# A decoder trunk on one core: the query norm carried into the exponential's scale, and an output projection of 512 columns

## The chip, the cores and the metric

The kernel runs as one program on one core of one Trainium2 chip. The metric is the time of one execution on the device in microseconds (us); the time before is the median of three runs. The profile is one execution of the same program taken by the hardware profiler. Engines are named as in the profile: PE is the matrix engine, PEld its loading of weights, DVE the vector engine, ACT the scalar engine, POOL the third elementwise engine, SP the queue that issues nearly all transfers.

## The reference

512 prompt rows and 32 sample rows (8 sequences of 4 new tokens) go through a trunk of two layers, D = 1024, 8 heads of 128, FFN width 2816. Layer 0 is FFN, gated token mixer, FFN, gated embedding; after it a shared K/V and a log-forget value for each head and row are made. Layer 1 has attention in the mixer's place. The change lies in layer 1's attention:

```python
q = rmsnorm((xn @ att_w_q[j]).reshape(bsz, L, N_HEADS, HEAD_DIM), q_norm[j])   # norm over each head's 128
...
s = jnp.einsum('bqhd,bkhd->bhqk', qb, k).astype(jnp.float32) * scale           # scale = 128 ** -0.5
s = s + cq[..., :, None] - csum[..., None, :]                                  # summed log-forget
s = jnp.where(causal[None, None], s, -jnp.inf)
p = jax.nn.softmax(s, axis=-1).astype(v.dtype)
o = jnp.einsum('bhqk,bkhd->bqhd', p, v)
mix = o.reshape(bsz, L, D_ATT) @ att_w_o[j]
h = h + mix                                                                    # then FFN on rmsnorm(h)
```

The sample rows attend to 256 cached rows each, in pages, and to their own 4. All of it is float32 at the accuracy of float32.

## The kernel before

Activations stand transposed: `h[c]` holds 128 features (chunk c of 8) by 544 columns, 512 of the prompt and 32 of the sample. Two chunks share one tile (`hp`). A weight matrix comes in units of 128 x 1024, each with a load on SP and a split into two reduced-precision halves, `hi` by an ACT cast (L242) and `lo` by a DVE subtraction (L243). A product is then three matmuls, hi·hi, hi·lo and lo·hi (L286, L290, L292 in `mm`), and these run on two column halves of 272 (`HT`). A product of the sample with raw float32 operands, 32 weight columns wide, stands four abreast in the array (for example L904 in the K/V stage). `prepare` splits a weight unit two or three units ahead of its use.

Layer 1's attention (`attention`) is a list of steps, the string `ORDER`, executed in that order in the source; each step is a letter and a number. A scheduler of the language then places each instruction on its engine by a timeline of its own, so that the order on an engine is not that of the source where dependencies leave room; an engine runs its list strictly in order. The steps:

- `q` head h's query tile (48 matmuls over 8 chunks), evicted by DVE (L1112) with the row norm of the stream, then squared on ACT (L788). `s` adds up the squares of four heads (L796), takes the root, and sends the rows to DRAM and back as a tile over all partitions; `n` multiplies q by it on DVE (L1122); `p` splits q into two halves.
- `f` fetches K and V of a head; `a` (`qk`) is its scores in four blocks of 128 queries, the log-forget terms entering as one more matmul (L1173) of two operands `L` and `R`; behind it stand the maximum (L1188, DVE), the exponential (L1189, ACT), the reciprocal (L1190) and the scaling of the rows (L1192, L1194). `t` transposes the weights (L1204), `v` is the product with V (L1223 to L1225).
- `K`, `V` load cache pages; `z`, `S`, `T`, `P`, `U`, `O` are the sample's attention: `S` scores (L1250), `T` transposes, `P` the product with the cached V (L1289, L1296), picked out by heads on DVE (L1303, L1305), `U` a transpose back (L1309, copied at L1312), `O` the split into the columns of the sample in `o` (L1320, L1321).
- `h` (`project_half`) is the output projection of the first 272 columns for two chunks and four heads at a time, `o` (`project`) that of the other 272 columns for one chunk and all heads. Both read `att_w_o`, in two layouts (`woh`, `wo`), so that its 4 MB are loaded and split twice.

When a chunk of `h` is done, `on_chunk` prepares it for the next FFN: `prep` (L342 on ACT, L343 on DVE), the square for the norm (L369 on ACT, added up on POOL at L371). The next FFN begins with four plain query-like tiles (L286 to L292) and goes on with products of combined blocks (L540) that need `forms`, sums of a pair of chunks (L352, L330 on ACT; L356, L358, L359, L331 on DVE). `early={5: 0, 6: 1}` makes two of the four forms when chunks 5 and 6 are done. PSUM is held in three double tiles (`ps`) and two single ones (`pb`).

## Time and profile before

| what | value |
|---|---|
| runs | 1926.22 us median (1925.88, 1926.22, 1927.91) |
| the profiled execution | 1926.16 us, span 1924.4 us, TensorE clock granted 1.0 |
| PE matmul | 1903.1 us busy (99%), 16508 instructions |
| DVE / ACT / POOL | 1457.2 (76%) / 949.1 (49%) / 142.2 us (7%) |
| chain that ended last | PE 89%, DVE 6%, ACT 3% |
| layer 1's attention | the norm sums of its first query tile (L408) at 1355.2 us, the next FFN's first matmul at 1518.3 us |

The chain of work follows PE from one end to the other. Matmuls overlap: a matmul's record lasts longer than the distance to the next one's start, so what a matmul costs is read from two starts, not from one record's length. Where a stage keeps PE busy without a gap, its time is the number of its matmuls by that distance; where PE waits, the view of waits names for what.

### The profile page before, as it was taken

The numbers are of one execution on the slowest core, as the hardware profiler recorded it, in microseconds if no ns is written. First come the engines' busy times: TensorE is split into PE (matmuls) and PEld (weight loads), VectorE is DVE, ScalarE is ACT, GpSimd is POOL, SyncE is SP. The second block draws the span as 40 slices with busy tenths as digits, with TensorE's granted clock in tenths as the row PEclk, the third lists the DMA queues.
The fourth block names the chain that finished last, engine by engine and source line by source line (L and its number), as shares of the span: only waits on it lengthen the run. The fifth ranks groups of instructions, "written<-read, shape, count | busy, mean of one in ns | idle before, by whom it ended". The sixth has DMA issues, their size and how long they took to land.

```text
span 1924.4 us, 39011 instructions
## 1 busy us (share of the span) xinstructions
PE 1903.1 (99%) x16508; PEld 1869.2 (97%) x16508; DVE 1457.2 (76%) x1801; ACT 949.1 (49%) x1398; POOL 142.2 (7%) x190
## 2 busy tenths in 40 slices
PE   9999999999999999999999999999999999999999
PEld 8999999999999999999999999999977899999999
DVE  7987877556788887767578887876476888878774
ACT  7544434424554544454466444444374754444461
POOL 0000000400100000023000000002131300000020
PEclk9999999999999999999999999999999999999999
DMA  5323235203223233431484232324769332332431
GB/s 197 92 98 125 88 115 165 90 26 110 89 88 116 94 113 121 130 112 50 150 304 148 97 129 71 128 96 128 227 212 333 101 109 86 107 113 86 143 106 47
DMA packets 98048, 237.62 MB, mean 123 GB/s; under 512 B 12130, under 2 KB 29826, under 8 KB 97874
## 3 DMA queue, kind: packets, MB, share of 16 engines
q1 hardware_dynamic: 97730, 235.09, 36.9%
q8 instruction: 130, 2.13, 0.5%
q14 instruction: 44, 0.36, 0.1%
q10 hardware_dynamic: 144, 0.04, 0.0%
HBM read 218.65 MB, written 16.44 MB: 122 GB/s over the span
## 4 chain that ended last, share of the span: by engine, by line
PE 89%; DVE 6%; ACT 3%; issue 1%; DMA 1%; POOL 0%; SPq 0%; ACTq 0%; DVEq 0%; POOLq 0%
PE ps L540 31%; PE ps L286 15%; PE ps L292 15%; PE ps L290 15%; PE pb L540 5%; DVE big L243 1%; ACT big L242 1%; DVE big L227 1%; PE ps L893 1%; PE ps L894 1%; PE ps L895 1%; DMA big<-in_w13p 1%; DVE big L331 0%; DVE big L498 0%; PE ps L1289 0%
## 5 line engine op out<-in xcount | busy, mean ns | idle before, releaser
L540 PE MATMUL ps<-big,big 128*128 128x272 f32 x5616 | 668.7, 279 | 4.0 <-ACT tmp L548 2.6
L540 PEld LDWEIGHTS ps<-big,big 128*128 128x128 f32 x5616 | 658.5, 189 | 5.0 <-ACT tmp L548 3.2
L243 DVE TENSOR_TENSOR big<-big,big 128x1024 fp32r<-128x1024 f32 (+2 forms) x507 | 582.3, 1152 | 87.1 <-ACT big L242 86.4
L242 ACT CAST big<-big 128x1024 fp32r<-128x1024 f32 (+2 forms) x507 | 482.5, 972 | 326.1 <-DVE big L227 253.2
L286 PE MATMUL ps<-big,big 128*128 128x272 f32 x2668 | 530.3, 280 | 3.6 <-ACT big L242 2.3
L292 PE MATMUL ps<-big,big 128*128 128x272 f32 x2668 | 527.6, 279 | 1.4 <-DVE big L243 1.3
L290 PE MATMUL ps<-big,big 128*128 128x272 f32 x2668 | 527.5, 279 | 0.5 <-DVE big L343 0.5
L286 PEld LDWEIGHTS ps<-big,big 128*128 128x128 f32 x2668 | 407.3, 189 | 8.2 <-ACT big L242 5.2
L292 PEld LDWEIGHTS ps<-big,big 128*128 128x128 f32 x2668 | 406.8, 189 | 2.8 <-DVE big L243 2.4
L290 PEld LDWEIGHTS ps<-big,big 128*128 128x128 f32 x2668 | 406.8, 189 | 0.9 <-DVE big L343 0.9
L371 POOL TENSOR_TENSOR st<-st,tmp 128x544 f32<-128x544 f32 (+1 forms) x63 | 87.6, 1391 | 1485.0 <-ACT tmp L369 1484.8
L227 DVE TENSOR_TENSOR big<-big,big 128x1024 f32<-128x1024 f32 x156 | 190.1, 1218 | 0.0
L579 DVE SCALAR_TENSOR_TENSOR big<-ps,big 128x544 f32<-128x544 f32 x128 | 92.4, 722 | 104.1 <-PE ps L292 103.2
L548 ACT COPY tmp<-ps 128x544 f32<-128x544 f32 x117 | 71.5, 611 | 111.3 <-PE ps L540 111.2
L498 DVE TENSOR_TENSOR big<-big,st 128x1088 f32<-128x1088 f32 x88 | 113.2, 1288 | 3.4 <-ACT big L562 2.0
L540 PE MATMUL pb<-big,big 128*128 128x272 f32 x936 | 114.8, 279 | 0.0
L540 PEld LDWEIGHTS pb<-big,big 128*128 128x128 f32 x936 | 111.3, 189 | 0.0
L501 ACT ACTIVATE big<-big 128x544 f32<-128x544 f32 x88 | 57.8, 659 | 87.7 <-DVE big L498 87.6
L342 ACT ACTIVATE big<-big,gains 128x544 fp32r<-128x544 f32 (+1 forms) x80 | 55.5, 702 | 90.0 <-DVE big L579 55.1
L331 DVE TENSOR_TENSOR big<-big,big 128x544 fp32r<-128x544 f32 (+1 forms) x112 | 79.3, 714 | 22.8 <-ACT big L330 22.6
L343 DVE SCALAR_TENSOR_TENSOR big<-big,gains,big 128x544 fp32r<-128x544 f32 (+1 forms) x80 | 64.7, 816 | 23.6 <-ACT big L342 23.4
L330 ACT CAST big<-big 128x544 fp32r<-128x544 f32 (+1 forms) x112 | 71.2, 644 | 12.0 <-DVE big L504 7.4
(218 smaller groups left out, 1385.8 us busy)
## 6 DMA issues: line engine op xcount, KB each, us to landing
big<-in_w SPq DMA_DIRECT2D x156, 512.0 KB
big<-in_w2b SPq DMA_DIRECT2D x96, 384.0 KB
big<-in_w13p SPq DMA_DIRECT2D x16, 512.0 KB
big<-in_w2a SPq DMA_DIRECT2D x16, 512.0 KB
big<-in_win SPq DMA_DIRECT2D x16, 512.0 KB
big<-in_wg SPq DMA_DIRECT2D x16, 512.0 KB
big<-in_ck SPq DMA_DIRECT2D x16, 512.0 KB
big<-in_cv SPq DMA_DIRECT2D x16, 512.0 KB
```

The costliest lines, as they stand in the source:

```text
L227: self.nc.vector.tensor_tensor(t, a, b, ALU.add if op == "+" else ALU.subtract)
L242: self.nc.scalar.copy(hi[:, c], src[:, c])
L243: self.nc.vector.tensor_tensor(lo[:, c], src[:, c], hi[:, c].bitcast(F32), ALU.subtract)
L286: i = nc.tensor.matmul(o, wh, xh[:, b], start=s, stop=False)
L290: nc.tensor.matmul(o, wh, xl[:, b], start=False, stop=False)
L292: nc.tensor.matmul(o, wl, xh[:, b], start=False, stop=e)
L331: self.nc.vector.tensor_tensor(pair[:, 1, cols], src, pair[:, 0, cols].bitcast(F32), ALU.subtract)
L371: nc.gpsimd.tensor_tensor(acc[:, cols], acc[:, cols], sq, ALU.add)
L498: tt(g, g, rstd.unsqueeze(1).broadcast_to([P, 2, T]), ALU.mult)
L540: nc.tensor.matmul(turns(dst[w]), a[:, c], woven(b), start=k in "152" and kp == 0 and n == 0, stop=kp == NKP - 1 and n == 2, skip_group_ch ...
L548: nc.scalar.copy(t["r" + k], t["C" if k == "5" else "A"])
L579: nc.vector.scalar_tensor_tensor(halves(h[c]), whole(out), 0.5, halves(h[c]), ALU.mult, ALU.add)
```

## The change

- The query norm is not applied to q. q goes unnormed, with the gain of the norm alone, into the scores (`prep` in place of `split_pair`). Each query row's factor enters at the exponential as a scale, and the maximum is multiplied by it before. The log-forget terms, which must not be scaled, are divided by it: operand `L` now carries the root of the row and `R` the terms (their parts are exchanged).
- The factor is made in columns: the sums of squares (`s`) are copied to a tile, turned by four transposes (`root`, L1131), and a root is computed on 16 columns by an integer estimate and three rounds of Newton on DVE (L1136 to L1150). `rows` spreads it, transposes it back (L1159) and copies it (L1160) to `L`. For heads 0 to 3, `root` and `rows` are called from within the query tiles 4 and 5, ahead of the last chunk; for heads 4 to 7 they are steps `c1` and `r1`. The trip through DRAM and steps `n`, `z` and `O` are gone; the sample's queries are copied and squared on POOL as each head's tile is evicted.
- Maxima, reciprocals and scalings come for two query blocks at once.
- The projection of the prompt runs on 512 columns, two chunks and four heads at a time (`project`, L1364 to L1368), with one layout of `att_w_o`, loaded and split once. The sample's 32 rows are projected with the raw weights in float32, four abreast (`sample_project`, steps `g`, L1405), copied by ACT (L1409), summed over the four groups by two small matmuls (`sample_add`, steps `e`, L1415) and added by DVE (L1418).
- A chunk counts as done when both parts are in; `on_chunk` then prepares all 544 columns at once. `early={1: 0, 3: 1, 5: 2}`: three forms.
- `ORDER` is written anew: head 0's scores come after query tile 5, and query tiles 6 and 7 stand between the first heads' scores.

```diff
-q0 K3 K2 K0 q1 q2 q3 K1 s0123 n2 n3 n1 q4 f1 p1 q5 q6 f0 n0 q7 p2 p0 f3 f2 a0 s4567 p3 t0 a1 v0 a2
...
-V3 v5 a6 x V2 h10 t6 a7 V4 S1 t7 T0 v6 V0 V1 v7 h20 V6 h30 T1 P0 h01 U0 P1 O0 h11 h21 U1 O1 h31 o0 o1 o2
-o3 o4 o5 o6 o7
+q0 K3 K2 K0 q1 q2 q3 s0 f0 q4 p0 f1 q5 a0 p1 K1 q6 t0 f2 a1 p2 q7 s1 v0 t1 c1 f3 a2 p3 v1 S0 t2 r1 a3
...
+t7 T0 V0 V1 v7 h20 V6 T1
+P0 h30 U0 P1 h01 U1 h110 g0 g1 h111 e0 e1 g2 g3 h210 e2 e3 h211 h31
```

```diff
+                p = self.tile_mm(xs, mid={4: lambda: root(0), 5: lambda: rows(0)}.get(h))
...
+        def stat(g):
+            box["row", g] = row = self.tmp()
+            for a, t in enumerate(self.head_stat([sqs.pop(4 * g + j) for j in range(4)])):
+                nc.scalar.copy(row[:, a * HT:(a + 1) * HT], t[:, :HT])
+        def root(g):
+            dve, n, t, row = nc.vector, 18 if g else 16, self.pb(), box.pop(("row", g))
+            for i in range(4):
+                nc.tensor.transpose(t[:, i * P:i * P + P], row[:, i * P:i * P + P], self.ident)
+            for k in range(2 * g):
+                nc.tensor.matmul(t[:, 1 + k:2 + k], ss[k], self.ones[:, 0:1], start=True, stop=True, skip_group_check=True)
...
+            for _ in range(3):
+                dve.tensor_tensor(u, y, y, ALU.mult)
+                dve.scalar_tensor_tensor(u, u, -0.5, x, ALU.mult, ALU.mult)
+                dve.scalar_tensor_tensor(y, u, 1.5, y, ALU.add, ALU.mult)
...
+            for k, part in enumerate((hi.bitcast(F32), u)):
+                dve.tensor_copy(v[:, :, :, 2 * k:2 * k + 2], part.unsqueeze(2).unsqueeze(3).broadcast_to([P, 16, NH, 2]))
+        def rows(g):
+            w, t = box.pop(("w", g)), self.pb()
+            for i in range(4):
+                nc.tensor.transpose(t[:, i * P:i * P + P], w[:, i * P:i * P + P], self.ident)
+            nc.scalar.copy(self.L[:, g, :SEQ], t)
...
-                nc.tensor.matmul(into, self.L[h % 4][:, qs], blocks_woven(self.R[:, 0, :w]), start=True, stop=False)
+                nc.tensor.matmul(into, self.L[:, h // 4, qs], blocks_woven(self.R[h % 4][:, :w]), start=True, stop=False)
...
-                nc.scalar.activation(blocks_halves(p[:, :w]), blocks_unwoven(sc), AF.Exp, bias=m, accum_out=l)
+                nc.scalar.activation(blocks_halves(p[:, :w]), blocks_unwoven(sc), AF.Exp, bias=m2[:, k], scale=r2[:, k],
+                                     accum_out=l2[:, k])
...
+        def project(c, part, only=None):
+            if only != 1:
+                st["sum", c, part] = self.ps()
+            p = st["sum", c, part]
+            hi, lo, _ = weights(c, part)
+            for a in range(2) if only is None else (only,):
+                w = slice(4 * P * a, 4 * P * a + 4 * P)
+                product(p[:, a, :], (hi[:, w], lo[:, w]), range(4 * part, 4 * part + 4))
+                if part == 1:
+                    out = halves(h_out[2 * c + a][:, :SEQ])
+                    nc.vector.tensor_tensor(out, unwoven(p[:, a, :]), out, ALU.add)
+                    done(c, a)
...
+        def sample_project(c):
+            st["part", c] = t = self.pb()
+            for part in range(2):
+                w = weights(c, part)[2].rearrange("p (a n m) -> p n a m", a=2, n=4)
+                for n in range(4):
+                    nc.tensor.matmul(t[32 * n:32 * n + 32, :2 * P].rearrange("p (a m) -> p a m", a=2),
+                                     st["os"][:, 4 * part + n, :], w[:, n], start=part == 0, stop=part == 1,
+                                     skip_group_check=True)
+            st["own", c] = s = self.tmp()[:, :2 * P]
+            nc.scalar.copy(s, t[:, :2 * P])
+        def sample_add(c):
+            s, t = st.pop(("own", c)), st.pop(("part", c))
+            for a in range(2):
+                nc.tensor.matmul(t[:, 2 * P + NS * a:2 * P + NS * a + NS], s[:, P * a:P * a + P],
+                                 self.c[:, C_SUM:C_SUM + NS], start=True, stop=True, skip_group_check=True)
+            out = self.hp[c][:, :, SEQ:]
+            nc.vector.tensor_tensor(out, t[:, 2 * P:2 * P + 2 * NS].rearrange("p (a t) -> p a t", a=2), out, ALU.add)
+            done(c, 0, 1)
...
-        on, nxt = self.next_norm(h, G_FFN2 + 8, early={5: 0, 6: 1})
+        on, nxt = self.next_norm(h, G_FFN2 + 8, early={1: 0, 3: 1, 5: 2})
```

Ahead of the attention, the two sides issue the same matmuls in the same order.

Three places of the new order matter below. In the rows that follow, a name's number is the buffer.

The first place is on PE where head 0's scores begin. Before, the first matmul of the scores of head 0 (L1173, the log-forget term) stands among the matmuls of a query tile:

```order
L286 MATMUL ps_16809<-big_15947,big_16679 128x272 x2
L290 MATMUL ps_16809<-big_15947,big_16679 128x272 x2
L1173 MATMUL ps_16875<-big_16229,big_16232 128x256
L292 MATMUL ps_16809<-big_15947,big_16680 128x272 x2
L286 MATMUL ps_16809<-big_15965,big_16679 128x272 x2
```

Now the transposes of `rows` (L1159, which read `tmp_16654`) stand behind the last matmul of query tile 5 (`ps_16684`), and the scores (L1210 is the log-forget term, whose weights are `L`, `big_16223`) directly behind them:

```order
L286 MATMUL ps_16684<-big_16216,big_16506 128x272 x2
L290 MATMUL ps_16684<-big_16216,big_16506 128x272 x2
L292 MATMUL ps_16684<-big_16216,big_16507 128x272 x2
L1159 MATMUL pb_16727<-consts,tmp_16654 128x128 x4
L1210 MATMUL ps_16746<-big_16225,big_16223 128x256
```

On DVE the last rows that make `tmp_16654` (L1154) have the eviction of query tile 5 (L1107, from `ps_16684`) between them:

```order
L1148 TENSOR_TENSOR cols<-cols 128x16
L1149 CAST cols<-cols 128x16
L1150 TENSOR_TENSOR cols<-cols 128x16
L1154 COPY tmp_16654<-cols 128x128x2
L1107 TENSOR_TENSOR big_16663<-ps_16684,st_16294 128x544
L1154 COPY tmp_16654<-cols 128x128x2
L343 SCALAR_TENSOR_TENSOR big_16793<-big_16304,gains,big_16793 128x512
```

So four transposes and the copy to `L` now stand between the query tile and the scores, and one of their operands is complete only after the eviction of that same tile.

The second place is on DVE behind the sample's product with V. Before, the picking of the second group (L1303, L1305) follows the copy of the first transpose back (L1312) directly:

```order
L1312 COPY tmp_18336<-pb_18334 128x128
L1303 TENSOR_SCALAR tmp_18363<-ps_18338,consts 128x128
L1305 SCALAR_TENSOR_TENSOR tmp_18363<-ps_18338,consts,tmp_18363 128x128 x7
L1355 TENSOR_TENSOR big_93<-ps_18388,big_93 128x2x272
L1355 TENSOR_TENSOR big_94<-ps_18432,big_94 128x2x272
```

Now an addition of the projection (L1393) stands between its parts, and on PE 13 matmuls of 512 columns stand between the two transposes back (L1346), where 36 of 272 stood before:

```order
L1350 COPY tmp_18288<-pb_18286 128x4x8x4
L1340 TENSOR_SCALAR tmp_18315<-ps_18290,consts 128x128
L1393 TENSOR_TENSOR big_92<-ps_18324,big_92 128x512
L1342 SCALAR_TENSOR_TENSOR tmp_18315<-ps_18290,consts,tmp_18315 128x128 x7
L1393 TENSOR_TENSOR big_92<-ps_18324,big_92 128x512
```

So the second transpose back has less time on PE and one DVE instruction more ahead of it.

The third place is on ACT where the next FFN's first weight unit is cast (L242). Before, that cast stands among the work of the last chunks' second halves (`big_94` is chunks 4 and 5, `big_95` chunks 6 and 7):

```order
L342 ACTIVATE big_18470<-big_94,gains 128x272
L369 ACTIVATE tmp_18757<-big_94 128x272
L330 CAST big_18765<-tmp_18763 128x544
L330 CAST big_18766<-tmp_18764 128x544
L242 CAST big_18775<-big_18691 128x1024
L342 ACTIVATE big_18528<-big_95,gains 128x272
```

Now it comes behind two chunks' preparation, a form, and the copies for the last two sums of the sample (L1409), with chunks 4 to 7 still to be prepared:

```order
L342 ACTIVATE big_18446<-big_93,gains 128x544
L342 ACTIVATE big_18452<-big_93,gains 128x544
L352 ACTIVATE big_18458<-big_93,gains 128x544 x2
L330 CAST big_18463<-tmp_18461 128x544
L1409 COPY tmp_18487<-pb_18472 128x256
L1409 COPY tmp_18504<-pb_18489 128x256
L330 CAST big_18464<-tmp_18462 128x544
L242 CAST big_18477<-big_18329 128x1024
L369 ACTIVATE tmp_18526<-big_94 128x544
```

On PE the last matmuls of the projection, the two pairs L1415 that read `tmp_18487` and `tmp_18504`, and the first matmul of the FFN, which reads `big_18477`, follow one another directly.

More of the change, by code (lines that the diff above doesn't have):

```diff
@@ L1332, in product @@
                 c = slice(P * n, P * n + P)
-                s, e = n == 0, n == len(ks) - 1
-                i = nc.tensor.matmul(turns(out), hi[:, c], woven(o[k][:, 0, hs]), start=s, stop=False)
-                if pin and s:
+                xh, xl = (woven(o[k][:, x, :SEQ]) for x in range(2))
+                i = nc.tensor.matmul(turns(out), hi[:, c], xh, start=n == 0, stop=False)
+                if pin and n == 0:
                     self.tc.keep_in_program_order(i)
-                if not late:
-                    nc.tensor.matmul(turns(out), hi[:, c], woven(o[k][:, 1, hs]), start=False, stop=False)
@@ new lines, in product, with weights, done @@
+                nc.tensor.matmul(turns(out), lo[:, c], xh, start=False, stop=n == len(ks) - 1)
+        def weights(c, part):
+            if ("w", c, part) not in st:
+                hi, lo = self.unit()
+                st["w", c, part] = hi, lo, self.raws[self.pieces[self.p_next - 1]["src"][0]]
+            return st["w", c, part]
+        def done(c, *chunks):
+            for a in chunks:
+                st["done", c, a] = st.get(("done", c, a), 0) + 1
+                if st["done", c, a] == 2:
+                    on_chunk(2 * c + a)
@@ L1371, in attention @@
+        do = dict(q=tile, s=stat, c=root, r=rows, f=fetch, p=prep_q, a=qk, t=turn, v=pv, K=self.load_k, V=self.load_v,
+                  S=sample_qk, T=sample_turn, P=sample_pv, U=sample_back, x=load_vs, h=project,
+                  g=sample_project, e=sample_add)
         for step in ORDER.split():
```

163 lines of the change are left out of this document (73 added, 90 removed).

## The prediction

> **What bounds the kernel now.** The page first: how busy PE is, and whether any other engine comes near it.
>
> ```profile
> span 1924.4 us, 39011 instructions
> PE 1903.1 (99%) x16508; PEld 1869.2 (97%) x16508; DVE 1457.2 (76%) x1801; ACT 949.1 (49%) x1398; POOL 142.2 (7%) x190
> ```
>
> PE is without work for about 21 us of 1924.4. A change can win what of that idleness lies in its own stage, and what it takes off PE itself; anything else is hidden. So the second view is busy time by stretches (core time, then busy us of PE, PEld, DVE, ACT, POOL). The first row is another FFN's beginning, in layer 0; the others run through layer 1's attention and the start of its second FFN.
>
> ```profile
> 540.00:564.00 24.00, 23.27 (x201) 23.04 (x200) 23.49 (x30) 14.84 (x21) 0.00 (x0) 1.00 0.41 132
> 1344.00:1392.00 48.00, 47.71 (x404) 45.13 (x403) 22.39 (x30) 16.68 (x23) 8.39 (x18) 1.00 0.70 210
> 1392.00:1416.00 24.00, 20.58 (x138) 17.17 (x138) 15.73 (x41) 16.81 (x45) 7.56 (x11) 1.00 0.37 127
> 1416.00:1484.00 68.00, 67.15 (x711) 54.99 (x710) 47.92 (x111) 41.63 (x106) 18.75 (x40) 1.00 0.99 327
> 1484.00:1518.00 34.00, 32.20 (x279) 30.99 (x265) 28.71 (x46) 22.12 (x53) 14.22 (x27) 1.00 0.40 135
> 1518.00:1544.00 26.00, 24.29 (x201) 23.37 (x200) 21.77 (x31) 19.33 (x30) 1.90 (x2) 1.00 0.29 101
> 1544.00:1572.00 28.00, 25.34 (x214) 24.77 (x213) 24.91 (x26) 15.95 (x22) 0.00 (x0) 1.00 0.24 76
> ```
>
> Clock column: 1.00 throughout. PE's idleness (first two numbers subtracted) is 0.29 + 3.42 + 0.85 = 4.56 up to 1484, 1.80 to 1518, 1.71 to 1544 and 2.66 to 1572: 10.73 us. That is all that better order can give back. The waits of PE in 1380 to 1572 (us in total, times, longest) say what ended it:
>
> ```profile
> PE ps L1173 <- ACT tmp L1189: 2.6, 4, 1.3
> PE ps L540 <- ACT tmp L548: 1.7, 2, 1.3
> PE ps L292 <- DVE big L243: 1.3, 3, 0.5
> PE ps L1341 <- POOL big L1321: 1.2, 1, 1.2
> ```
>
> The first heads' scores wait for PSUM that exponentials still hold; the FFN's start waits for weight splits and evictions; the last projection waits for POOL's split of the sample's `o`, which the change drops.
>
> **PE's own work.** Prices are distances between starts:
>
> ```profile
> 1369.80 0.40 PE L290 MATMUL ps<-big,big 128*128 128x272 f32 x2
> 1370.03 0.40 PE L292 MATMUL ps<-big,big 128*128 128x272 f32 x2
> ...
> 1399.56 0.38 PE L1174 MATMUL ps<-big,big 128*128 128x512 f32 x1
> 1399.78 0.38 PE L1175 MATMUL ps<-big,big 128*128 128x512 f32 x1
> 1400.00 0.38 PE L1176 MATMUL ps<-big,big 128*128 128x512 f32 x1
> ...
> 978.66 0.28 PE L895 MATMUL ps<-big,big 128*128 128x256 f32 x1
> 978.86 1.07 PE L904 MATMUL pb<-big,xraw 128*32 128x256 f32 x16
> 979.86 0.38 PE L893 MATMUL ps<-big,big 128*128 128x256 f32 x1
> ...
> 927.88 1.18 PE L977 MATMUL pb<-big,tmp 128*128 128x8 f32 x10
> 928.91 0.36 PE L894 MATMUL ps<-big,big 128*128 128x256 f32 x1
> ...
> 1417.83 0.93 PE L1204 MATMUL ps<-consts,tmp 128*128 128x128 f32 x7
> 1418.51 0.46 PE L1223 MATMUL pb<-big,big 128*128 128x512 f32 x1
> ```
>
> - Projection: 384 matmuls of 272 at 0.23 / 2 = 0.116 give 44.5 us; 192 of 512 at 0.22 (0.2165 over the run of them) give 41.6. **-2.9**. The columns fall from 384 x 272 to 192 x 512, by 6%, because the sample's leave.
> - `sample_project`: the sample's columns come back as 32 raw float32 products of 256 columns, four abreast. L904 is the same shape: 16 records are 8 products and take 1.00 us, with about 0.2 around them for coming and going. They stand in two blocks of 16: 2 x (2.0 + 0.2) = **+4.4**.
> - `sample_add`: 8 float32 products with 128 weight columns and 32 moving ones. Nearest is L977, 5 products in 1.03: 0.2 each, 1.6, and 0.2 for changes: **+1.8**. `root`'s two products of one column, the same price: **+0.4**.
> - 16 transposes in four blocks: 7 in 0.68, so 0.1 each, and 0.1 a block for changing: **+2.0**.
>
> PE gets 5.7 us more to do. Bounds: 4.5 if block changes cost nothing, 7 if each small float32 product costs 0.3.
>
> The Trainium skill would price the first item otherwise. Its page "TensorE: Matmul & The Clock Gate", section "Back-to-back issue gap", gives 131 ns for each 512-column matmul in a sustained stream of weight loads and matmuls; by it the projection would be 25.1 us, and the sum 16.4 lower. The trace disagrees: the three L1174 to L1176 rows, each with its own weights, stand 0.22 apart; the measurement decides.
>
> **Waits.** Prices from rows of the stage 1344 to 1572 (mean ns before the last bar), and the rows around the transpose back of the sample:
>
> ```profile
> L1112 DVE TENSOR_TENSOR big<-ps,st 128x544 f32<-128x544 f32 x8 | 5.7, 722 | 10.3 <-PE ps L292 10.3
> L331 DVE TENSOR_TENSOR big<-pb,big 128x256 fp32r<-128x256 f32 x8 | 3.3, 414 | 0.0
> L1228 ACT CAST big<-pb 128x512 fp32r<-128x512 f32 x8 | 4.6, 582 | 5.7 <-PE pb L1225 5.7
> L243 DVE TENSOR_TENSOR big<-big,big 128x1024 fp32r<-128x1024 f32 x36 | 44.5, 1240 | 6.9 <-ACT big L242 6.5 <-DMA big<-in_cv 0.3
> L242 ACT CAST big<-big 128x1024 fp32r<-128x1024 f32 x36 | 37.0, 1040 | 9.5 <-DVE big L227 7.9 <-PE ps L540 1.6
> L352 ACT ACTIVATE big<-big,gains 128x544 f32<-128x544 f32 x8 | 5.5, 739 | 0.0
> L330 ACT CAST big<-tmp 128x544 fp32r<-128x544 f32 x8 | 5.1, 646 | 4.3 <-DVE tmp L359 3.1 <-DVE tmp L356 1.0
> ...
> 1485.90 0.27 PE L1309 MATMUL pb<-consts,tmp 128*128 128x128 f32 x1
> ...
> 1486.21 0.29 DVE L1312 COPY tmp<-pb 128x128 f32<-128x128 f32 x1 [2.07 <-PE pb L1309]
> 1486.42 0.34 DVE L1303 TENSOR_SCALAR tmp<-ps,consts 128x128 f32<-128x128 f32 x1
> 1486.79 2.67 DVE L1305 SCALAR_TENSOR_TENSOR tmp<-ps,consts,tmp 128x128 f32<-128x128 f32 x7
> 1489.38 0.71 DVE L1355 TENSOR_TENSOR big<-ps,big 128x544 f32<-128x544 f32 x1
> ```
>
> - First heads. Query tiles 6 and 7 (5.6 us each) now cover the exponentials of heads 0 and 1, so the 2.6 us at L1173 go. In their place head 0 waits once: `rows`' transposes need a DVE copy that stands behind the eviction of query tile 5 (0.3 from PE to DVE, as 1485.90 to 1486.21; 0.72; the copy like L331, 0.41), and the scores behind them need L1160 (0.3 and 0.58): 2.2 us that nothing covers, since PE's next instruction is the waiting one. With ACT behind on head 1's transposed weights I put 3.6 us of idleness where 4.56 stood: **-1.0** (ends -3 and +1).
> - Transpose back. From the first L1309 to the end of the second picking DVE needed 1489.38 - 1485.90 = 3.5 us, and 36 matmuls covered it. Now an addition of 512 columns (0.7) stands within and 13 matmuls, 2.8 us, cover 4.2: **+1.4**.
> - The end of the projection. Counting from the second transpose back, PE has 72 projection matmuls, 4.4 and 1.8: 21.8 us. Chunks 0 and 1 are done only at `e0`, behind 36 of the 72 and a block of L1405: 10 us in. From then ACT must prepare and square four chunks (8 at some 0.7, like its other passes over 544 columns), make two forms (4 x 0.74 and 4 x 0.65), copy twice for the sample (0.4 each) and cast a weight unit (1.04): 13 us and its waits on DVE, against 11 us of PE. By walking it PE stands about 1.5 us at `e2`, 2.5 at the FFN's first weight unit, 1.5 at later chunks and units: 5.5. Without the mutual waits of ACT and DVE 1.5. Before, this stretch idled 1.80 + 1.71 = 3.5. I take 4.0, nearer the walk: **+0.5** (ends -2 and +2).
> - The FFN's combined products. Eight splits of `wo` no longer compete just ahead, and three forms of four are made earlier. The same setting in layer 0 idles 0.73 (first row of the stretches) where 2.66 stood; the bunched chunks keep DVE late, so I take 1.0: **-1.7** (ends -2 and 0).
> - At nothing: ACT loses eight casts and the split of the sample's `o`, DVE eight norms and eight splits, SP 8 loads of 512 KB and the trip of the norms; all lie under PE. If that cover were gone, DVE's part (8 x 1.24 + 8 x 0.72, about 16 us) would count, which is the first rival. POOL gets 32 small operations for the sample's copies and squares in a stretch where it was busy 8.39 of 48; the second `root`, the only reader in a hurry, is some 5 us of PE work behind the last query tile. The longer softmax (maximum, product, then exponential) is behind fillers. The weight loads are halved in number and hidden under 0.22.
>
> Sum: 5.7 - 1.0 + 1.4 + 0.5 - 1.7 = **+4.9 us**. Against the profiled execution's 1926.16 (span 1924.4 and 1.8 around it, 0.06 under the median) this is 1931.1; I forecast 1931.0, slower by 0.25%. About 0.2%, 3.85 us, is what a measurement of this kernel can tell from no change.
>
> **Rivals.**
> - DVE, not PE, sets the stretch 1488 to 1572 (21.77 of 26 and 24.91 of 28 busy), so that its lighter load returns time there. Place: the FFN's start. It decides if the idleness after the change falls under 10.73 - 5.7 = 5.0 us, less than half. If the whole tail idles like layer 0's (0.7) and the first heads at the 2.2 of the one wait, the time is 1926.2 + 5.7 - 10.7 + 2.9 = 1924.1: no change. For it: the FFN's waits are on splits and evictions. Against it: chunks end within 10 us, not spread over 20 as before. Beyond it, at 1922, nearly everything would have to vanish.
> - The bunching costs the walk's full price: ACT and DVE alternate through forms with each waiting for the other, and the third and fourth tile wait too. +2 there, +2 in the first heads, FFN unchanged (+1.7): 1937.
> - In a dense run the matmul of 512 columns keeps a shorter distance than in the scores, at best that of 272 columns: 192 x 0.116 = 22.3 in place of 41.6, and 1911.7. The three rows at 0.22 speak against it; 1 in 100. The Trainium skill's figure above would put this case at 1914.6.
>
> **How the numbers follow.** Forecast case (1928 to 1934.5) 0.52; first rival 0.30, a third of it below 1922.4; second rival 0.17; third 0.01. Slower by over 0.2% means above 1930.1: 0.39 of the forecast case's 0.52, and the 0.17: 0.56. Faster: 0.11. Same: 0.33. The range 1922.5 to 1938 leaves out 0.11 below and some 0.05 above; the forecast case's own is 1928 to 1934.5.
>
> **What would show it.** 512-column matmuls of the projection 0.216 apart; L1405 in two blocks of about 2 us; PE idle over 1 us at L1159 or L1210 by DVE L1154 and ACT L1160; about 1.4 at the second L1346, by DVE L1342; PE waiting at L1415 for ACT L1409 and at the FFN's first L286 or L292 for L242, L243; and under 1 us idle at L540. I am wrong if the idleness from query tile 0 to the combined products falls under 5 us, or if the small float32 blocks cost PE less than 4 us.

## The result and the profile after

The changed kernel took 1941.43 us (median of six runs, 1939.82 to 1943.65), the kernel before 1926.66 (median of six): ratio 1.0077, 95% interval 1.0065 to 1.0088. It is slower by 14.8 us where 4.9 were forecast. The direction was right, the size was not, and 1941 lies outside the range.

The page of the profiled execution, and its row in the view of spans and clocks:

```profile
span 1939.9 us, 38708 instructions
PE 1914.9 (99%) x16416; PEld 1871.8 (96%) x16416; DVE 1443.7 (74%) x1803; ACT 940.8 (48%) x1363; POOL 144.1 (7%) x183
```

```profile
core 0: 1939.9 us, clock 0.996
```

PE is busy for 11.8 us longer than before and idles for 25.0 where it idled 21.3. And the granted clock is no longer 1.0. To see where, the span is cut at two events that both kernels have: the last L408 of the first query tile, and the FFN's first L286 behind the projection. Busy time by stretches, of the kernel before:

```profile
1355.35:1518.32 162.97, 156.60 (x1418) 137.14 (x1416) 111.20 (x221) 93.39 (x221) 41.98 (x84) 1.00 0.72 234
1518.32:1924.39 406.07, 397.80 (x3417) 396.21 (x3416) 312.23 (x359) 190.21 (x256) 12.91 (x9) 1.00 0.30 100
```

and of the changed one (the last three numbers of a row are granted clock, DMA share, GB/s; the rows of 3.41 and 6.83 us are explained below):

```profile
1354.95:1531.63 176.68, 163.97 (x1326) 135.03 (x1324) 97.85 (x228) 84.74 (x187) 38.83 (x76) 0.99 0.57 188
1531.63:1939.91 408.28, 401.70 (x3416) 400.50 (x3416) 312.68 (x355) 191.39 (x256) 18.15 (x11) 0.99 0.29 95
...
1416.00:1484.00 68.00, 63.75 (x583) 54.72 (x583) 40.55 (x107) 40.92 (x106) 17.91 (x34) 0.98 0.84 275
...
1527.44:1530.85 3.41, 1.08 (x8) 0.97 (x8) 3.06 (x8) 2.05 (x5) 0.00 (x0) 1.00 0.53 213
1530.85:1537.68 6.83, 6.05 (x25) 5.74 (x26) 5.79 (x6) 5.34 (x8) 3.97 (x2) 0.50 0.01 2
1411.39:1414.80 3.41, 1.80 (x16) 1.50 (x15) 2.16 (x6) 2.35 (x6) 0.00 (x0) 1.00 0.45 171
1414.80:1418.21 3.41, 3.41 (x12) 3.14 (x12) 2.16 (x11) 0.27 (x1) 0.00 (x0) 0.50 0.02 5
1575.25:1578.66 3.41, 1.35 (x12) 1.18 (x11) 3.41 (x5) 1.46 (x2) 0.00 (x0) 1.00 0.00 0
1578.66:1582.07 3.41, 3.41 (x17) 3.41 (x16) 3.41 (x5) 1.78 (x3) 0.00 (x0) 0.50 0.00 0
```

The stretch from query tile 0 to the FFN grew by 13.7 us, the rest by 2.2; ahead of it the changed kernel was 0.4 quicker. Of the 13.7, PE idles 12.71 in place of 6.37 (length less busy time), which is 6.3; PE is busy 7.4 longer, of which 1.7 is the half clock at 1414.80 (half of 3.41); 5.7 is work.

Three times TensorE runs at half its clock: for 3.41, 6.83 and 3.41 us, each time behind a stretch of 3.41 us in which PE was busy for no more than 1.8. The starts lie on one grid: 1530.85 - 1414.80 is 34 times 3.413, 1578.66 - 1530.85 is 14 times. The matmuls show it: L1270 and L1271, of 512 columns, stand 0.42 apart in it.

```profile
1413.23 0.66 PE L1131 MATMUL pb<-consts,tmp 128*128 128x128 f32 x4 [1.07 <-DVE big L1275]
1413.72 0.50 PE L1133 MATMUL pb<-ones,big 128*128 128x1 f32 x4
1414.76 0.73 PE L1269 MATMUL pb<-big,big 128*128 128x512 f32 x1 [0.54 <-DVE cols L1138]
1415.29 0.63 PE L1270 MATMUL pb<-big,big 128*128 128x512 f32 x1
1415.71 0.63 PE L1271 MATMUL pb<-big,big 128*128 128x512 f32 x1
```

The waits of PE from 1380 to 1600 (us in total, times, longest):

```profile
PE pb L1415 <- ACT tmp L1409: 2.4, 1, 2.4
PE ps L540 <- DVE big L557: 2.1, 1, 2.1
PE ps L286 <- ACT big L242: 1.5, 1, 1.5
PE ps L1250 <- ACT tmp L1241: 1.4, 3, 0.8
PE pb L1269 <- ACT big L330: 1.2, 1, 1.2
PE pb L1159 <- DVE tmp L1154: 1.1, 1, 1.1
PE pb L1131 <- DVE big L1275: 1.1, 1, 1.1
PE ps L1364 <- DVE big L1393: 1.0, 1, 1.0
PE pb L1269 <- ACT tmp L1317: 0.8, 1, 0.8
PE ps L1210 <- POOL big L1171: 0.8, 1, 0.8
```

The waits of heads 0 and 1 for exponentials (2.6 at L1173) are gone; those at the first `rows` (L1159, L1210: 1.9; the view names POOL's copy L1171 for the second, but that had ended at 1384.12, while the copy to `L`, L1160, ended at 1384.54 and L1210 began at 1384.64, so it was L1160), at the second `root` (L1131 and the L1269 behind it: 1.6) and of the later heads stand in their place. From 1416 to 1484 alone PE idles 4.25 us, where it idled 0.85. At the projection's end it waits 2.4 and 1.5, and at the combined products 2.1.

### The profile page after: what moved, and what is told of

Read it like the earlier page. It is cut to its first block, busy times and chain, and to the rows that moved or that the text cites. A ratio compares the mean times of both kernels' runs of the same rounds, so it can differ in the third digit from the quotient of the medians.

```text
span 1939.9 us, 38708 instructions
## 1 busy us (share of the span) xinstructions
PE 1914.9 (99%) x16416; PEld 1871.8 (96%) x16416; DVE 1443.7 (74%) x1803; ACT 940.8 (48%) x1363; POOL 144.1 (7%) x183
## 4 chain that ended last, share of the span: by engine, by line
PE 91%; DVE 5%; ACT 2%; issue 1%; DMA 0%; SPq 0%; POOL 0%; ACTq 0%; DVEq 0%; POOLq 0%
PE ps L540 31%; PE ps L286 15%; PE ps L292 15%; PE ps L290 15%; PE pb L540 5%; DVE big L243 1%; ACT big L242 1%; PE ps L893 1%; PE ps L894 1%; PE ps L895 1%; DVE big L227 1%; PE ps L1364 1%; DVE big L331 1%; PE ps L1367 1%; PE ps L1368 1%
## 5 line engine op out<-in xcount | busy, mean ns | idle before, releaser
L243 DVE TENSOR_TENSOR big<-big,big 128x1024 fp32r<-128x1024 f32 (+2 forms) x499 | 572.1, 1150 | 87.5 <-ACT big L242 86.9
L242 ACT CAST big<-big 128x1024 fp32r<-128x1024 f32 (+2 forms) x499 | 474.5, 971 | 329.8 <-DVE big L227 255.4
L286 PE MATMUL ps<-big,big 128*128 128x272 f32 x2668 | 531.4, 280 | 3.8 <-ACT big L242 2.4
L292 PE MATMUL ps<-big,big 128*128 128x272 f32 x2668 | 528.7, 280 | 0.5 <-DVE big L243 0.5
L286 PEld LDWEIGHTS ps<-big,big 128*128 128x128 f32 x2668 | 408.4, 189 | 8.2 <-ACT big L242 4.9
L292 PEld LDWEIGHTS ps<-big,big 128*128 128x128 f32 x2668 | 407.8, 189 | 1.6 <-DVE big L243 1.2
L371 POOL TENSOR_TENSOR st<-st,tmp 128x544 f32<-128x544 f32 x56 | 86.6, 1546 | 1500.7 <-ACT tmp L369 1500.4
L331 DVE TENSOR_TENSOR big<-big,big 128x544 fp32r<-128x544 f32 (+1 forms) x104 | 73.6, 716 | 20.4 <-ACT big L330 20.4
L330 ACT CAST big<-big 128x544 fp32r<-128x544 f32 (+1 forms) x104 | 66.2, 645 | 8.5 <-DVE big L504 7.4
```

The costliest lines, as they stand in the source:

```text
L242: self.nc.scalar.copy(hi[:, c], src[:, c])
L243: self.nc.vector.tensor_tensor(lo[:, c], src[:, c], hi[:, c].bitcast(F32), ALU.subtract)
L286: i = nc.tensor.matmul(o, wh, xh[:, b], start=s, stop=False)
L292: nc.tensor.matmul(o, wl, xh[:, b], start=False, stop=e)
L331: self.nc.vector.tensor_tensor(pair[:, 1, cols], src, pair[:, 0, cols].bitcast(F32), ALU.subtract)
L371: nc.gpsimd.tensor_tensor(acc[:, cols], acc[:, cols], sq, ALU.add)
```

## The experiments

Times are medians of five runs or more (e5: one execution, for its trace) beside runs of the kernel before (medians 1925.99 to 1926.87); a ratio's 95% interval reaches some 0.0013, or 2.5 us, to each side. Some experiments are compared with one another and not with the kernel before; there "clear" means that all runs of the one lie beyond all runs of the other. A trace is one execution, and the half clock falls on other places from one execution to the next. Diffs show a line of `ORDER` only as far as it changes. "Attention" is the stretch from the last L408 to the FFN's first L286 (176.7 us in the changed kernel), "rest" the one from there to the end (408.3).

### Which half of the change

e4 has norm and heads of the changed kernel, and `product`, `project_half`, `project`, `sample_out`, both layouts of the weights and `early` of the kernel before:

```diff
-t7 T0 V0 V1 v7 h20 V6 T1
-P0 h30 U0 P1 h01 U1 h110 g0 g1 h111 e0 e1 g2 g3 h210 e2 e3 h211 h31
+t7 T0 V0 V1 v7 h20 V6 h30 T1 P0 h01 U0 P1 O0 h11 h21 U1 O1 h31 o0 o1 o2
+o3 o4 o5 o6 o7
```

> The norm half of the change with the projection, sample split, steps O and o and early={5: 0, 6: 1} of the kernel before. By the trace of the changed kernel: PE work -3.3 (projection and sample 47.8 against 44.5), the idleness from the end of the heads on 6.2 as in the kernel before against 7.5, no half clock at the end of the projection and at the combined products (-3.0 - 1.7): 1932.1 (theory: over half of the loss lies in the projection half). Rival: the first heads carry the loss, since a lighter ACT and DVE at the end was worth more than it cost: 1938 or slower.

Measured 1936.59. e6 is the other half on the kernel before, with the changed kernel's `project`, `sample_project`, `sample_add` and `early`:

```diff
-v7 h20 V6 h30 T1 P0 h01 U0 P1 O0 h11 h21 U1 O1 h31 o0 o1 o2
-o3 o4 o5 o6 o7
+v7 h20 V6 T1
+P0 h30 U0 P1 h01 U1 h110 g0 g1 h111 e0 e1 g2 g3 h210 e2 e3 h211 h31
```

> The kernel before with the projection half of the change: 512 columns, sample_project, sample_add, its end of ORDER from V6 on, early={1: 0, 3: 1, 5: 2}; norm and heads as before. If the halves add up (theory 1): 1941.4 - 1936.6 = 4.8 above 1926.0, 1930.8. Rival 1 (the projection half loses by itself what the trace of the changed kernel shows from the transposes back on: 1.9 of PE work, 1.3 of waits, and up to 4.7 at half clock): 1934. Rival 2 (the waits at its end come from the norm half's later heads): 1928 or less.

Measured 1932.58. The two stretches of e4, then of e6:

```profile
1356.51:1527.68 171.17, 160.48 (x1438) 138.96 (x1436) 107.34 (x240) 96.44 (x223) 49.25 (x101) 1.00 0.64 210
1527.68:1934.35 406.67, 397.80 (x3417) 396.21 (x3416) 312.20 (x359) 190.30 (x256) 12.90 (x9) 1.00 0.30 99
```

```profile
1354.85:1521.61 166.76, 158.01 (x1306) 131.51 (x1304) 101.05 (x209) 81.79 (x185) 30.31 (x59) 1.00 0.65 212
1521.61:1930.78 409.17, 400.74 (x3416) 399.24 (x3416) 312.58 (x355) 191.38 (x256) 18.17 (x11) 0.99 0.29 95
```

The norm half adds 8.2 us to the attention (3.9 busy, 4.3 idle) and nothing to the rest beyond the span's last 0.6; the projection half adds 3.8 (1.4 busy, 2.4 idle) and 3.1 to the rest. With 1.7 of half clock that is the 13.7. The losses in whole runs, 10.6 and 6.4, add up to 17.0, against 14.8. So my theory for e4, that over half lay in the projection, fell: the norm half is the larger. Its transposes and roots had been forecast with 2.4 us of PE work, where 3.9 came, and its waits with a gain.

### The half clock: what brings it, what it costs

e1 puts matmuls into the wait at the projection's end:

```diff
+            with self.tc.issue_after(st["last"].ins):
+                for _ in range(10):
+                    nc.tensor.matmul(t[:, 0, :], o[0][:, 0, :P], o[1][:, 0, :SEQ], start=True, stop=True)
```

> Ten matmuls of 512 columns, whose result nobody reads, stand behind the last projection matmul, where PE waits 2.40 us for ACT L1409; at 0.2165 they take 2.2 us, so they lie inside that wait, and the work that PE waits for is the same. Theory G (the clock: the trace of the changed kernel shows TensorE at half clock for 3.41, 6.83 and 3.41 us, each time behind a stretch of 3.41 us in which PE was busy for under 1.9 us): the 6.83 us at half clock that begin at the end of the projection do not occur, and the 6.05 us of work in them take half as long: -3.0 us, 1938.4. Theory W (the waits alone cost, and the clock follows from nothing that PE does there): no gain, 1941.4, or up to 0.5 more, and the half clock stays.

Measured 1942.39. The wait is filled (L1425) and the half clock at that place is gone, as theory G said. But nothing is gained: from 1531.60 to 1538.40, where the FFN begins, the clock is whole, and PE idles 2.1 us. Rows of the timeline, and of two stretches:

```profile
1416.93 0.38 PE L1270 MATMUL pb<-big,big 128*128 128x512 f32 x1
1417.15 0.38 PE L1271 MATMUL pb<-big,big 128*128 128x512 f32 x1
...
1528.29 2.45 PE L1425 MATMUL ps<-big,big 128*128 128x512 f32 x10
1530.85 1.08 PE L1415 MATMUL pb<-consts,tmp 128*128 128x32 f32 x8
1533.46 0.50 PE L286 MATMUL ps<-big,big 128*128 128x272 f32 x2 [1.53 <-ACT big L242]
```

```profile
1531.60:1538.40 6.80, 4.74 (x38) 4.43 (x38) 5.41 (x7) 6.20 (x9) 3.98 (x2) 1.00 0.11 44
1533.46:1942.30 408.84, 399.73 (x3416) 397.95 (x3416) 312.62 (x355) 191.36 (x256) 18.15 (x11) 1.00 0.28 95
```

The rest is 408.84 long, 408.28 before the edit: PE is busy 2.0 us less in it and idles 2.5 more (9.1 for 6.6). Half a clock in this stretch, which ACT and DVE set, cost nothing; theory G holds for what brings the half clock and fails for its price there. In this execution the grid lay elsewhere: no half clock at the second `root`, and from L1131 to head 2's first L1250 it took 8.1 us (1415.11 to 1423.20) where the changed kernel took 9.8 (1413.23 to 1422.99). That is the 1.7, where PE was the bound. But two others came, behind the first `rows` and at 1460, which ate it up.

e5 puts gaps of 22 lengths between groups of 48 matmuls, in a tail behind the kernel before:

```diff
+            for _ in range(48):
+                nc.tensor.matmul(t[:, 0, :384], self.identr, cur[:, :384], start=True, stop=True)
+            nc.vector.tensor_copy(x[:, :384], t[:, 0, :384])
+            for _ in range(j * 13 % 22):
+                nc.vector.tensor_copy(x[:, :64], t[:, 0, :64])
```

> The kernel before with a tail behind its last instruction: 44 groups of 48 matmuls of 384 columns (some 7.9 us each), with a chain of 1 to 22 small DVE copies between groups, so that PE waits from under 1 to over 3 us in 22 lengths, each twice. It leaves the result as it is; only its trace is read. Theory G1 (the clock is decided at the end of each stretch of 3.41 us on a fixed grid, by how long PE was busy in it; in the changed kernel 1.08, 1.35 and 1.81 us brought the half clock and 2.08 did not): stretches with under 1.8 us of work are followed by 3.41 us at half clock, those with over 2.1 are not, so that waits from some 1.4 us on can bring it, by where they fall on the grid, and waits of 1.0 never do. Theory G2 (one wait must last a whole stretch of 3.41 us): no half clock behind waits under 3.4 us.

Stretches on the grid and the one behind each (PE busy is the second number, the clock the third from the end):

```profile
2179.24:2182.65 3.41, 1.47 (x8) 1.34 (x8) 1.68 (x6) 0.00 (x0) 0.00 (x0) 1.00 0.02 5
2182.65:2186.06 3.41, 3.41 (x12) 3.41 (x12) 0.00 (x0) 0.00 (x0) 0.00 (x0) 0.50 0.00 0
2435.24:2438.65 3.41, 1.62 (x9) 1.63 (x10) 1.52 (x7) 0.00 (x0) 0.00 (x0) 1.00 0.00 0
2438.65:2442.06 3.41, 3.41 (x22) 3.41 (x21) 0.00 (x0) 0.00 (x0) 0.00 (x0) 1.00 0.00 0
2421.58:2425.00 3.42, 2.64 (x8) 2.64 (x9) 0.66 (x3) 0.00 (x0) 0.00 (x0) 0.50 0.00 0
2425.00:2428.41 3.41, 3.41 (x12) 3.41 (x12) 0.00 (x0) 0.00 (x0) 0.00 (x0) 0.50 0.00 0
2486.44:2489.85 3.41, 2.92 (x9) 2.93 (x10) 0.40 (x2) 0.00 (x0) 0.00 (x0) 0.50 0.00 0
2489.85:2493.26 3.41, 3.41 (x22) 3.41 (x21) 0.00 (x0) 0.00 (x0) 0.00 (x0) 1.00 0.00 0
```

In this tail of equal matmuls G1 holds and G2 falls: 1.47 us of work brought it and 1.62 did not. The shortest wait behind which it came was 1.94 us; none of the ten waits up to 1.68 brought it.

### The first heads

e2 puts `rows(0)` into query tile 6 and head 0's scores behind it.

```diff
-                p = self.tile_mm(xs, mid={4: lambda: root(0), 5: lambda: rows(0)}.get(h))
+                p = self.tile_mm(xs, mid={4: lambda: root(0), 6: lambda: rows(0)}.get(h))
-q5 a0 p1 K1 q6 t0 f2 a1 p2 q7
+q5 p1 K1 q6 a0 f2 q7 t0 a1 p2
```

> rows(0) ahead of the last chunk of query tile 6 in place of 5, and head 0's scores behind tile 6. The waits at L1159 and L1210 (1.11 and 0.78 us) are covered by the tile in both theories. Theory 1 (they cost what they last): -1.9 us, 1939.5. Rival (the first heads have a fixed amount of uncovered softmax, and tile 6 is then missing as cover between heads 0 and 1): the idleness comes back at heads 1 and 2, 1941.4 or slower.

Measured 1937.90, 3.5 less (the runs of the two overlap by 0.4). The attention is 4.3 shorter: 1.7 of it idleness, 1.7 the half clock that did not occur behind the second `root` in this execution, the rest PE work. So theory 1 holds for the idleness.

```profile
1354.73:1527.12 172.39, 161.38 (x1326) 133.37 (x1324) 97.75 (x228) 84.56 (x187) 39.44 (x76) 1.00 0.59 192
1527.12:1935.41 408.29, 401.65 (x3416) 400.57 (x3416) 312.67 (x355) 191.50 (x256) 18.19 (x11) 0.99 0.28 95
```

e7 gives e4 the order of the later heads of the kernel before:

```diff
-p4 f4 v2 K5 t3 a4 f5 p5 K6 v3 f6 h00 p6 V5 f7 t4 a5 K7 K4 v4 p7 V7 V3 h10 t5 a6 x V2 v5 S1 t6 a7 V4 v6
-t7 T0 V0 V1 v7
+p4 f4 v2 K5 f5 p5 K6 t3 a4 v3 f6 h00 p6 V5 f7 a5 K7 t4 K4 v4 t5 p7 V7 V3 v5 a6 x V2 h10 t6 a7 V4 S1
+t7 T0 v6 V0 V1 v7
```

> e4 (norm half alone) with the order of the kernel before from head 4 on: the next head's scores ahead of the transposes of a head's weights (a5 t4 v4 t5 ... in place of t4 a5 v4 ... t5). Theory H (the order of the heads makes the waits at L1250, L1210 and L1270, 3.6 us in e4, where the kernel before had some 1.9 from head 1 on): -2.0, 1934.6. Rival (they come from the two single PSUM tiles that root, rows, sums, transposes and products with V take in turn, whatever the order): within 0.7 of 1936.6.

Measured 1938.94, no better than e4's 1936.59: its profiled attention idles 11.8 us, e4's 10.7, and runs 13.7 us at half clock, e4's none. Theory H falls. e8 is e7 with the edit of e2:

> e7 with rows(0) in query tile 6 and head 0's scores behind it, as in e2. e2 gave 3.5 us, of which 1.7 in its trace was idleness, 1.7 half clock behind the second root, and 0.9 fewer changes at the sums. Theory (the first heads' waits at rows(0) and root(1) cost by themselves): 1.9 below e7 if no half clock is in play in e7, up to 3.5 if one is. Rival (in e2 only the changed phase of the half clock gained): no gain over e7.

Measured 1934.42, 4.5 under e7 and clear of it. In the two traces the attention idles 2.0 us less (9.8 for 11.8), about what the first `rows` waits, and runs 6.8 us at half clock in place of 13.7: the first `rows` costs what it lasts, and more where the half clock follows. e9 moves the second `root` of e2:

```diff
-v0 t1 c1 f3 a2 p3 v1 S0 t2 r1 a3
-p4 f4 v2 K5 t3 a4
+v0 t1 f3 a2 p3 v1 t2 a3 c1 S0
+p4 f4 v2 r1 K5 t3 a4
```

> e2 with the second root behind head 3's scores and the transposes of head 2 (t2 a3 c1 S0 p4 f4 v2 r1 in place of c1 f3 a2 p3 v1 S0 t2 r1 a3). In the trace of the changed kernel head 2's reciprocal (L1235) at 1422.34 stands on DVE behind the last operations of this root (L1142 to L1154), though its exponentials ended at 1420.09, and L1250 waits for it; the root's PSUM tile also makes L1131 and the next product with V wait. Theory R (the second root, where it stands, costs these waits): 1.2 to 1.9 less idleness from query tile 7 to head 4, 1936.3. Rival (any place among the heads costs the same): the waits reappear at S0, r1 or head 4, 1937.9.

Measured 1936.78, 1.1 less, which is not clear; the attention is 1.4 shorter, but only 0.5 of that is idleness, since the sample's scores now wait 1.0 at L1286 behind the root's products (L1133). e13 takes the PSUM of `root` and `rows` in e2 from the other pool:

```diff
-            w, t = box.pop(("w", g)), self.pb()
+            w, t = box.pop(("w", g)), self.ps()[:, 0, :]
```

> e2 with the PSUM of root and rows in one of the three double tiles (ps) in place of the two single ones (pb). Theory Q (the single tiles, which the sums, root, rows, a head's transposes and its product with V take in turn, hold the heads up): the waits at L1131 (0.64) and at the next L1269 (0.54) go and no new one comes, -1.2, 1936.7. Rival (the double tiles, two for each head's scores and one for its transposes, are as short): the waits move to the scores or transposes, 1937.9 or slower.

Measured 1939.61, no gain: the waits moved to L796 (0.9, by the view for the product of maxima, L1228) and L1269 (1.2, for the copy of the sums, L1125), and the attention idles 11.7 where e2's idles 11.0. That it is slower is not clear, since its runs overlap e2's, and its trace has 3.41 us at half clock among the heads, e2's none. Theory Q falls: the waits at the second `root` went, and these two, of products that write the single tiles, came. e10 and e17 take the pairs out of the softmax of e2 (e10 the reciprocals, e17 the maxima as well):

```diff
-                    nc.vector.reciprocal(l2, l2)
+                nc.vector.reciprocal(l, l)
...
-                    for k in range(2):
-                        nc.vector.tensor_reduce(m2[:, k:k + 1], S[i // 2][:, k, :w + P * k], AX.X, ALU.max, negate=True)
-                    nc.vector.tensor_tensor(m2, m2, r2, ALU.mult)
+                nc.vector.tensor_reduce(m2[:, k], sc, AX.X, ALU.max, negate=True)
+                nc.vector.tensor_tensor(m2[:, k], m2[:, k], r2[:, k], ALU.mult)
```

> e2 with reciprocal and scaling for each block of 128 queries again, as in the kernel before, and maximum and product for two blocks as in the changed kernel. Theory P (the pairs make a head's first block wait for the second's exponential, some 0.7 us, and PE behind it at L1250): 1.0 less idleness at L1250 and L1210, 1936.9. Rival (the transposes wait for the last block, which a pair does not delay): within 0.5 of 1937.9.

> e10 with maximum, product with the factor and exponential for each block of 128 queries too, so that nothing of the softmax is paired. In the trace of the changed kernel ACT stood idle 2.37 us ahead of an exponential (L1231 at 1457.09) until the product of two maxima (L1228) came, with the split of the previous head's transposed weights (L330) behind it in its queue, and PE waited 1.19 at L1269 for that split. Theory S (the paired maxima make ACT, which runs in order, late for whatever stands behind): 1 to 2 less idleness among the heads, 1935.6. Rival (the longer chain is not at fault; the waits of the later heads come from where the scheduler put the splits): within 0.6 of e10's 1937.1.

Measured 1937.08 and 1942.19: the first is not clear of e2, the second is 5 us slower than the first. Theory S falls; single maxima added 2.1 of idleness to e10's attention (13.5 after 11.4). Which resource makes the later heads wait in the changed order stays open.

### The projection's end and the FFN's start

e3 sets `early={5: 0, 6: 1}` in the changed kernel, e16 sets `early={1: 0, 3: 1, 5: 2}` in the kernel before.

> early={5: 0, 6: 1} again in place of {1: 0, 3: 1, 5: 2}: no form is made before chunk 5. Theory B (ACT is late at the end of the projection because of the forms: one takes 2 x 0.74 and 2 x 0.65, 2.8 us on ACT): ACT comes to L1409 and to the first weight cast 2.8 us earlier or more, the waits of 2.40 and 1.53 shrink under 1.5 in sum and the half clock behind them goes (-2.4 - 3.0), while the combined products wait 1 to 2 us longer for their forms: -3.5, 1938. Rival (the eight preparations and squares alone keep ACT busy): the waits stay within 1 us of what they are and the time at 1941, or slower by the late forms.

> The kernel before with early={1: 0, 3: 1, 5: 2} alone. If the forms of the chunks are what the combined products waited for (2.66 us idle there): down to 1924.7. If ACT and DVE are full in that stretch, what the forms gain there is lost at the FFN's first tiles: 1925.7 to 1927.

Measured 1942.25 and 1930.27; the second is above what either theory gave. In e3 the waits of 2.4 and 1.5 are gone, as theory B said, and 4.1 us come back in the rest. (Seven matmuls of the FFN, some 0.8 us, stand ahead of the last sums L1415 in e3; its stretches are cut at the first L286 behind them.) In e16 the rest is 4.2 shorter and the attention 8.2 longer, 1.7 of it half clock: there the projection's weights wait behind the forms (L1334 for L242, 2.6). The two rows of e3, then of e16:

```profile
1355.18:1528.28 173.10, 164.31 (x1333) 136.01 (x1332) 96.21 (x219) 80.64 (x179) 39.25 (x76) 0.99 0.57 186
1528.28:1940.68 412.40, 400.92 (x3412) 398.40 (x3410) 316.48 (x365) 195.06 (x263) 16.93 (x11) 0.99 0.29 97
```

```profile
1354.95:1526.17 171.22, 159.20 (x1418) 139.02 (x1417) 117.82 (x232) 99.27 (x231) 42.52 (x85) 0.99 0.69 229
1526.17:1928.03 401.86, 396.60 (x3416) 395.95 (x3416) 304.97 (x348) 184.78 (x246) 12.07 (x8) 1.00 0.30 98
```

e11 puts the copy L1409 of e2 on DVE, e12 takes the squares out of e2 (`squares=(0,)` for this FFN alone):

```diff
-            nc.scalar.copy(s, t[:, :2 * P])
+            nc.vector.tensor_copy(s, t[:, :2 * P])
```

```diff
-            self.ssq(box["acc"], h[c], cols, first=c == 0)
+            if c in squares:
+                self.ssq(box["acc"], h[c], cols, first=c == 0)
```

> e2 with the copy of the sample's partial sums (L1409) on DVE in place of ACT. On ACT it stood 6 us behind its data, in the queue behind forms; on DVE the wait of 2.39 at L1415 shrinks under 1. Theory F (the start of the FFN is set by the total of ACT's and DVE's work on chunks, forms and weight units, not by this copy): the time comes back in the FFN's first tiles as in e1 and e3, within 0.8 of 1937.9. Rival (the copy's place in ACT's queue was the cause): 2.4 of wait and up to 1.7 of half clock less, 1935.5 or less.

> e2 without the squares of chunks 1 to 7 for the FFN's norm (its output is not the reference's): ACT loses 7 x 0.64 = 4.5 us between the projection and the FFN's norm, POOL 7 additions, DVE and PE nothing. Theory F (ACT and DVE in turn set the stretch from the projection's end to the combined products): the waits of 2.39 and 1.53 shrink by 2 or more and the stretch from the FFN's first matmul to the 400th L540, 88.6 in e2, does not grow by as much: -2.5, 1935.4 or less. Rival (DVE alone, or PE at half clock, sets it): under 0.7 less, 1937.2 or more.

Measured 1938.30 and 1932.94. On DVE the copy comes no earlier (2.7 at L1415): both engines are behind. Without 4.5 us of squares the time falls by 5.0, which is clear, and both stretches shrink, by 2.3 and 2.9:

```profile
1355.39:1525.53 170.14, 161.37 (x1326) 133.35 (x1325) 96.91 (x228) 83.08 (x184) 35.01 (x73) 1.00 0.59 195
1525.53:1930.93 405.40, 398.37 (x3416) 397.62 (x3416) 309.36 (x355) 189.04 (x252) 10.99 (x7) 0.99 0.29 96
```

In the attention this is idleness: 8.8 us where e2 has 11.0, with a wait of 0.5 at the sample's sums in place of 2.4. So ACT's work on the chunks is on the path there (POOL lost its additions too, but no wait of PE names POOL there). In the rest it is not idleness, which is 0.4 more, but PE's busy time, 3.3 less: the half clock lasts 3.41 us there in this trace and 9.7 in e2's, although the wait of 2.1 at the combined products is the same. How much of the 2.9 ACT's lighter work gave, and how much the place where the half clock fell, is not shown. e14 brings the same work forward:

```diff
-U1 h110 g0 g1 h111 e0 e1 g2 g3 h210 e2 e3 h211 h31
+U1 g0 g1 h110 e0 e1 h111 g2 g3 h210 e2 e3 h211 h31
```

> e2 with g0 g1 directly behind the second transpose back, ahead of h110, and e0 e1 ahead of h111: the same work in another order. Chunks 0 and 1 are complete some 2.6 us earlier, and ACT, which in the trace of the changed kernel idled 3.79 us ahead of its first L342, begins earlier. Theory F (the stretch is set by when ACT and DVE get the chunks, and by their work on them): the waits at the projection's end and in the FFN's start shrink by 2 to 3 us together, 1935.4. Rival (the last chunks, which the order does not bring forward, set it): 0.7 less at most, 1937.2 or more.

Measured 1935.81, 2.1 under e2 and clear of it, most of theory F's 2.5; the attention idles 8.7 where e2's idles 11.0. ACT's late start is part of it. e15 and e18 put edits together.

> e2 with the edits of e10 (single reciprocals), e13 and e14 together. If each of them brings what theories Q and F give, and e10 its 0.8: 1933.4. If the PSUM tiles only move the waits and the last chunks set the end: 1936.5 or more. Both are above the kernel before.

> e17 with the order of e14 (g0 g1 ahead of h110, e0 e1 ahead of h111). If what both bring adds up: 1935.6 - 2.1 = 1933.5 by theory S, 1935.0 by its rival. Under 1926.6 by neither.

Measured 1937.30 and 1938.33: both misses, as e13 and e17 already were. No version reached the kernel before.

## Why the prediction was right in its direction and wrong in its size

Against the profiled execution of before, 15.5 us are to be explained (1939.9 - 1924.4):

| term | forecast | measured |
|---|---|---|
| PE's own work | +5.7 | +5.7 |
| waits to the last head | -1.0 | +3.2 |
| second transpose back | +1.4 | +1.0 |
| end of the projection, and the FFN's start | +0.5 - 1.7 | +2.1 + 2.2 |
| half clock among the heads | none | +1.7 |
| ahead of the attention | none | -0.4 |

- PE's work was right as a sum, and partly by luck. 512 columns stand 0.215 apart, as forecast (1484.04, 1484.26, 1484.48 for L1367, L1368, L1364); the blocks of L1405 take 1.86 each (the first from 1510.75 to 1512.61; forecast 2.2). But by the halves the forecast was off both ways: e6's attention is busy 1.4 longer for the projection half where 3.3 (-2.9, 4.4 and 1.8) were forecast, e4's 3.9 for the norm half where 2.4 were. The two errors nearly cancel. Which matmuls make the norm half dearer stays open: its transposes and one-column products alone take some 2.6 by their starts in the changed kernel, near their 2.4.
- The first `rows` waited where the prediction said and for what it said, 1.9 for 2.2 (its five terms add up to 2.3). Query tiles 6 and 7 did cover heads 0 and 1. What failed is the rest of that term: 1.4 us had been put for all later heads. The second `root` was put at nothing because it stands some 5 us of PE work behind the last query tile. But it takes one of the two single PSUM tiles, so it waits itself for the addition L1275 that reads such a tile (1.1), and the next product with V waits for the root's reader L1138 (0.5). The other later heads idle 4.3 (1.4 + 1.2 + 0.8 + 0.4 and small ones in the waits). That the cover moved to the first heads is what they lack is not shown; no run took these waits away, and their cause stays open.
- At the second transpose back the size was near and the place wrong: both stand without a wait, and PE waits 1.0 for the addition L1393 that DVE does among the pickings.
- At the projection's end the walk (1.5 at L1415 and 2.5 at the FFN's first weights) was nearly what came (2.4 and 1.5). Idleness was not far off either: 4.4 (with 0.5 at L292) where the prediction says "I take 4.0", and 2.1 at the FFN's combined products where it says "I take 1.0". The step that failed is that both count PE's idleness alone. In the rest PE idles 1.7 less than before and is busy 3.9 longer; the half clock behind the waits, 9.5 us of it in the rest, makes 4.7 of that. e1 shows that without the first of these half clocks PE idles instead, so ACT's and DVE's work sets the time there and is what had to be priced; e3 and e16 show that early forms only move this work. Of the rivals the second (bunching at full price, 0.17) came nearest by its 1937, but of the waits at the third and fourth tile that it names only the 0.5 came. The first fell: the lighter DVE returned nothing.
- The half clock stood in no term. The Trainium skill, "TensorE: Matmul & The Clock Gate", section "What's actually happening", has a monitor that halves the clock by windows of 3.413 us on a free-running grid; the trace agrees in grid and lengths (3.41 and 6.83) and in the ratio (0.50). The prediction weighed that page of the Trainium skill for the price of a matmul and not for this, though its own walk put two waits side by side with only small products between them. Among the heads it cost 1.7, as the same stretch in e1 shows. What it cost at the combined products (3.41 us at half clock) no run tells by itself.
- The condition "wrong if the idleness falls under 5 us" was not met: it was 15.3 (12.71, and 0.49 and 2.06 in the FFN). The other, small float32 blocks under 4 us, is met by the two blocks of L1405 alone (3.7) and not together with the sums L1415 (1.8 by their starts).

## What to carry to other kernels

Price a stage by the engine that its buffers wait for: forms drawn forward on ACT delayed what stood behind them in its queue (e16: 4.2 us won, 8.2 lost), while removing work from ACT took time out (e12). A small chain that stands far from its inputs can still wait for a PSUM tile, and hold one that others need. And where waits leave PE little work in some 3.4 us (here under some 1.3 us, counted by the distances of starts), think of the half clock behind them, and add it to the sum if PE is the bound there.
